# Five steps of a two-layer encoder are issued at other places of the program: the key scale's sum, the queries' root, the seam's spread, the next layer's normalized x, the last reciprocals

## The chip, the cores and the metric

The kernel runs on one core of a Trainium2 chip. The metric is the device time of one execution in microseconds (us), the median of three runs. A core has engines with instruction streams of their own: TensorE (PE in the profile, its weight loads apart as PEld), VectorE (DVE), ScalarE (ACT), GpSimd (POOL) and SyncE (SP), which here issues DMA transfers. Matmul results go to PSUM, all other tiles lie in SBUF. An engine runs its own instructions in order and waits on semaphores for what others produce.

## The reference

Two layers of an encoder over 1024 tokens of width 1024. What bears on the change is cut out here.

```python
for l in range(DEPTH):                                  # 2 layers
    h = _rmsnorm(x, g_mix[l])
    p = h @ w_in[l]                                     # 384 query, 256 key/value, 32 rotary, 2 x 512 conv columns
    c_q = _rmsnorm(p[..., :o1], g_q[l])
    q = (c_q @ w_uq[l]).reshape(b, s, 8, 64 + 32)       # 64 plain, 32 rotary
    c_kv = _rmsnorm(p[..., o1:o2], g_kv[l])
    kv = (c_kv @ w_ukv[l]).reshape(b, s, 8, 64 + 64)    # keys, values
    k_rope = _apply_rope(p[..., o2:o3], cos, sin)       # one rotary key for all heads
    y_attn = _mla_attention(q_nope, q_rope, k_nope, k_rope, v)   # softmax(q k / sqrt(96)) v
    a, gt = jnp.split(p[..., o3:], 2, axis=-1)
    u = _dwconv(a * jax.nn.sigmoid(gt), ...)            # 31 taps along the tokens
    u = jax.nn.silu(_layernorm(u, ...))
    x = x + jnp.concatenate([y_attn, u], -1) @ w_o[l]
    h2 = _rmsnorm(x, g_ffn[l])
    zg, zv = jnp.split(_dwconv(h2 @ w_up[l], ...), 2, axis=-1)   # 3 taps, 2 x 2816 columns
    x = x + (jax.nn.silu(zg) * zv) @ w_down[l]
return _rmsnorm(x, g_final)
```

## The kernel before

Activations lie transposed, with channels on the 128 partitions and tokens along a row of 1024 (two halves of 512, each one bank of PSUM). A value that needs more digits than one type holds is split into an upper and a lower half (names ending in h and l, or the two planes of one tile): ACT writes the upper half, DVE subtracts it and writes the lower, and PE multiplies three of the four combinations.

Per layer there are four stages: `project` (all products with `w_in`, and the keys and queries of all heads), `attention`, the product with `w_o`, and the channel mixer with an `up` and a `down` product. The order in which the code issues instructions is the order in which each engine runs them; no scheduler moves them afterwards.

`project` writes this order with a small planner. `seq` is a list of sections, each one product on PE: a1, g2, a2, g3, a3 (convolution inputs), kv0, kv1 (keys and values, latent), kr (rotary key), q0, q1, q2 (queries, latent), k0 to k3 (keys), u0, u1 (rotary queries), n0 to n3 (plain queries). For each section it issues the product, and then `work(until)` issues the work of DVE and ACT that belongs to earlier sections: it holds a clock of its own for DVE and one for PE, takes from the list `active` the generator whose time has come, and where none is due takes a step of the convolution (`taps`, L2172, one multiply and add over a whole row). A generator yields its cost on DVE and the delay until its next step is due. After that `after()` of the section runs, which can start further generators, and the section's own eviction is launched.

The names around the change, in `project`:

- `keys_norm` spreads the key root over the partitions by eight PE transposes (rkv0s, L342), ACT copies them (L736), and DVE multiplies the two latent key tiles `ckv` by them (L739); `parts` then splits these into kvs_0 and kvs_1, which are the input of the sections k0 to k3.
- `key_scale` adds a few squares over the partitions by a matmul with ones (kt, L628, two small matmuls), and makes a power of two of them in a short chain on DVE (tiles qk, the last at L636). Then it launches `key_rope_end`, which splits the rotary key (krs; ACT at L782, DVE at L784) and sends it to DRAM (krd) through SP. The eviction of k0 to k3 (`key`, tiles ks, ACT at L806, DVE at L808) needs the scale too.
- `query_latent` of q0, q1, q2 scales the product (cq, L720), squares it on ACT (qss, L728), adds the squares up on DVE (the first sum at L283, the second at L285), and splits it (cqs, L794 and L796).
- `root("qss", ...)` runs behind section k2 in layer 0 and behind k3 in layer 1: eight transposes of the sum of squares (rq0t, L304), after which DVE forms the reciprocal root (`roots`). `queries_norm` spreads it (rq0s and rq1s, L342) and multiplies cos and sin by it.
- `product(..., between={k: f})` calls f ahead of the k-th of its moving tiles; each tile stands for six matmuls.

Layer 1 begins with `next_sections`, the seam: products of the new layer run over the first half of the tokens, (g0, a0, g1) x 8 steps, while the second half is normalized: `norm_root` behind step 15, `norm_spread` (rx_512s) and eight `norm_apply` (x at L1863, split into xs by ACT at L1864 and DVE at L1852) behind step 20. The first half is normalized earlier, by `put(...)` steps among the last steps of layer 0's `down` product (pd, L1666), whose inputs ab are split at L1655 (ACT) and L1656 (DVE) at the same time. In `attention` the softmax sums of the last pair of heads are inverted (rc, L2051) and spread by transposes (rc_1s).

Of the kernel before, what the change touches and what calls it, by code (L numbers as in the profile page):

```python
# [26 lines left out]
QL = 384  # L27
# [120 lines left out]
class Encoder:  # L148
# [406 lines left out]
    def next_sections(self, l, nxt, supply):  # L555
        names = ("g0", "a0", "g1")
        supply(-30.0)
        w = [e[0] for e in nxt["ready"]]
        self.norm_sums(l, nxt["x"], nxt, 1, (7,))
        for i in (2, 1):  # L560
            self.pp.tile([128, T], F32, name=f"skip{l}{i}", tag=f"w{i}", bufs=1)
        ps = [self.wide(f"p{n}{l}") for n in names]
        tiles = [(lambda k, t=t: (t[:, 0, k], t[:, 1, k])) for t in w]
        order = [(i, k) for ks in (range(6), range(6, 8)) for i in range(2) for k in ks] + [(2, k) for k in range(8)]
        for n, (i, k) in enumerate(order):
            self.partial(ps[i], tiles[i], nxt["hl"], k, (0,))
            if n == 15:
                self.norm_root(l, nxt, 1, self.bank)
            if n == 20:
                self.norm_spread(l, nxt, 1, self.bank)  # L570
                for m in range(8):
                    self.norm_apply(l, nxt["x"], nxt, 1, m)
        for k in range(8):
            for i in range(3):
                self.partial(ps[i], tiles[i], nxt["hl"], k, (1,))
        supply(-16.0)
        return nxt["hl"], None, dict(zip(names, ps))
# [13 lines left out]
    def project(self, l, carry):  # L591
# [3 lines left out]
        taps, active, u, conv, away, far_at = [], [], {}, {}, {}, {}  # L595
# [78 lines left out]
        def start(steps, wait=1.8):  # L674
            next(steps)
            active.append([clock["pe"] + wait, steps, 99])
# [56 lines left out]
        def keys_norm():  # L733
            r = st["rkv"] = self.blk(f"rkv{l}")
            for s, p in zip(HALVES, self.spread(rooted("kroot"), f"rkv{l}", HALVES, self.bank)):
                nc.scalar.copy(out=r[:, s], in_=p)  # L736
            yield 0.0, 1.8
            for j in range(2):
                nc.vector.tensor_tensor(out=ckv[j], in0=ckv[j], in1=r, op=ALU.mult)  # L739
                yield 1.25, 0.0  # L740
            both = [parts(ckv[j], f"kvs{l}_{j}", kvs, par[:, P_GKV + j:P_GKV + j + 1]) for j in range(2)]
            yield [next(p) for p in both][0]
            for p in both:
                yield from p
# [43 lines left out]
        def query_latent(j):  # L788
            yield from latent(f"q{j}", cq, "qss", j)
            yield from parts(cq[j], f"cqs{l}_{j}", cqs, par[:, P_GQ + j:P_GQ + j + 1])  # L790
# [71 lines left out]
        def inputs(name):  # L862
            if l:
                between = {4: lambda: start(keys_norm(), 6.5), 7: lambda: start(key_scale(), 9.6)} if name == "q1" else {}
                return lambda: self.product(ps[name], lambda k: (w[name][:, 0, k], w[name][:, 1, k]), hl, between=between)
            return lambda: self.product(ps[name], self.tiled(w[name]), hl)

        def ranked(group, j, n, name, moving):
            def run():
                pair = tuple(t[:, j] for t in w[group])  # L870
                self.product(ps[name], lambda k: tuple(t[:, k * 128:(k + 1) * 128] for t in pair), moving)
            return run

        def root(key, out, n, name):
# [29 lines left out]
            add(f"kv{j}", f"kv{j}", inputs(f"kv{j}"), lambda j=j: latent(f"kv{j}", ckv, "kss", j))  # L904
        add("kr", "kr", shared_key, key_rope)
        add("q0", "q0", inputs("q0"), lambda: query_latent(0), lambda: root("kss", "kroot", KVL, "rkv"))
        add("q1", "q1", inputs("q1"), lambda: query_latent(1), None if l else lambda: (start(keys_norm()), list(key_scale())))
        add("q2", "q2", inputs("q2"), lambda: query_latent(2))
        between = {2 + l: lambda: root("qss", "qroot", QL, "rq")}
        norm = lambda: start(queries_norm())  # L910
# [1 line left out]
            add(f"k{j}", "k", ranked("k", j, KVL, f"k{j}", kvs), lambda j=j: key(j), between.get(j))  # L912
        for i in range(2):
            held = lambda: launch(query_rope(0), len(seq) - 6)
            add(f"u{i}", "u2", ranked("u2", i, QL, f"u{i}", cqs), lambda i=i: query_rope(1) if i else iter(()), held if i else norm)
        scales = {1: lambda: self.weight_squares(l, w["v"], sc),
                  2: lambda: (st.update(scale=self.scales(l, sc)))}
        for j in range(4):
# [2 lines left out]
        times, starts, t = {}, {}, 0.0  # L921
# [633 lines left out]
    def down_steps(self, l, steps, put):  # L1555
# [201 lines left out]
        put(n4 + 2, 4, lambda: sums(1, range(4)))  # L1757
        put(n4 + 3, 0.5, lambda: self.norm_spread(l + 1, nxt, 0, other))
        for k in range(8):
            put(n4 + 4 + k * 3 // 4 if not last else n4 + 3 + k // 2, 4, lambda k=k: self.norm_apply(l + 1, x, nxt, 0, k))  # L1760

        def resume():
            if not last:
# [150 lines left out]
    def attention(self, l, u, conv, away, spill, kvs, loaded, ahead, wo, begun):  # L1914
# [134 lines left out]
        def inverse(c):  # L2049
            r = self.cp.tile([128, 4], F32, name=f"rc{l}_{c}", tag="rc", bufs=2)  # L2050
            nc.vector.reciprocal(out=r, in_=state[HEADS - 1]["sums"][:, c * 4:c * 4 + 4])  # L2051
            return r
# [48 lines left out]
        agenda[56].append(lambda: sums(last - 1, slice(0, 64), state[last - 1], state[last - 1]["y"], state[last - 1]["rb"]))  # L2101
        agenda[60].append(lambda: [self.load_y(l, begun["x"], 0, k) for k in range(2)])
        for c, when in enumerate((60, 62)):
            agenda[when].append(lambda c=c: inv.update({c: inverse(c)}))
            agenda[when + 1].append(lambda c=c: spread(c, inv.pop(c)))
        self.last_pair = lambda: finish(last, state_y(), 1)
        for i in range(1, 4):
# [11 lines left out]
        for n in range(-2, total + 2):  # L2119
            if n == total - 2:  # L2120
                expo(n + 1)
            for g, c in chain.get(n, ()):
                values(g, c, n)
            if n == total - 1:
# [212 lines left out]
```

## Time and profile before

| | us |
|---|---|
| runs, median (lowest, highest) | 2170.31 (2170.06, 2170.36) |
| profiled execution | 2170.75 |
| its span, from the first to the last instruction | 2169.0 |
| PE busy | 2159.5 |
| DVE busy | 1853.8 |
| ACT busy | 1475.9 |
| POOL busy | 532.2 |
| mean granted clock of PE | 1.000 |

The span is what the trace covers; 1.75 us of the profiled execution lie around it. Rows of the timeline give the start of an instruction or of several alike, their time together, the engine, the line in the kernel, the operation, out<-in by the program's names, and the shape; in square brackets stands how long the engine was idle just ahead of it, and what released it. In the list of waits, a row gives the engine and line that waited, whom it waited for, and then us in total, how often, and the longest. SPq is the queue of SP's DMA issues.

### The profile page before, as it was taken

To read this page: it belongs to the slowest core of one execution; us is meant where nothing else is said; L and a number is where in the kernel's file an instruction comes from. 1 tells how busy PE (TensorE), PEld (TensorE's weight loads), DVE (VectorE), ACT (ScalarE), POOL (GpSimd) and SP (SyncE) were. 2 spreads that over 40 slices of the span, in tenths; PEclk is the share of its full clock that TensorE was granted. 3 is DMA by queue.
4 is the path that set the end of the run, shared out by engine and by line. 5 is a ranking of instruction groups with operands and counts; after the bars stand their busy time and mean duration, and the time that the engine had idled before them with its cause. 6 is when DMAs were issued, how large, how long until landed. Compare 5 with 4: busy or idle time off the path is not lost.

```text
span 2169.0 us, 29811 instructions
## 1 busy us (share of the span) xinstructions
PE 2159.5 (100%) x10726; PEld 1178.7 (54%) x10726; DVE 1853.8 (85%) x2554; ACT 1475.9 (68%) x2204; POOL 532.2 (25%) x518
## 2 busy tenths in 40 slices
PE   9999999999999999999999999999999999999998
PEld 8887565754444444444444576567544444444445
DVE  6989999879988887887978789988898888878877
ACT  6455888746898889554534668886478888865544
POOL 1233767311121111000001157890111111110000
PEclk9999999999999999999999999999999999999999
DMA  6898878854689899555345678896646988856533
GB/s 193 185 188 211 168 144 170 257 148 116 140 240 261 223 282 272 185 180 181 124 160 107 150 181 166 172 211 198 170 98 166 262 242 241 239 138 220 188 114 122
DMA packets 161508, 402.00 MB, mean 185 GB/s; under 512 B 19872, under 2 KB 27920, under 8 KB 161360
## 3 DMA queue, kind: packets, MB, share of 16 engines
q1 hardware_dynamic: 104080, 266.79, 35.9%
q0 software_dynamic: 56992, 132.78, 33.8%
q8 instruction: 84, 1.38, 0.2%
q14 instruction: 64, 0.52, 0.1%
q10 hardware_dynamic: 288, 0.53, 0.1%
HBM read 270.75 MB, written 69.66 MB: 157 GB/s over the span
## 4 chain that ended last, share of the span: by engine, by line
PE 97%; ACT 2%; DVE 1%; issue 0%; DMA 0%; SPq 0%; DVEq 0%; ACTq 0%
PE p L1392 36%; PE pd L1666 18%; PE po L1098 7%; PE s L1951 7%; PE t L1991 5%; PE pq L265 3%; PE pa L265 3%; PE o L2013 2%; PE pkv L265 2%; PE pg L265 2%; PE pg L588 2%; PE pn L265 2%; PE o L2018 1%; PE pv L1927 1%; PE pk L265 1%; PE pa L588 1%
## 5 line engine op out<-in xcount | busy, mean ns | idle before, releaser
L1392 PE MATMUL p<-b,w 128*128 128x512 f16 x3696 | 800.2, 379 | 0.3
L1392 PEld LDWEIGHTS <-w 128*128 128x128 f16 x3696 | 358.9, 98 | 431.6 <-issue 0.8
L1666 PE MATMUL pd<-ab,wd 128*128 128x512 f16 (+1 forms) x1920 | 401.0, 371 | 0.4 <-DVE ab L1656 0.4
L1268 POOL DMA_DIRECT2D wu<-in_w_up x176 | 152.8, 882 | 770.0 <-DVE w L1356 583.5
L1666 PEld LDWEIGHTS <-wd 128*128 128x128 f16 x1920 | 187.9, 98 | 210.7 <-issue 0.9
L1951 PE MATMUL s<-k,q 96*128 96x512 f16 x768 | 186.9, 379 | 0.0
L1356 DVE SCALAR_TENSOR_TENSOR w<-wu,wf,w 128x512 f16<-128x512 f32 (+1 forms) x216 | 177.1, 834 | 5.1 <-ACT w L1353 4.9
L1994 DVE SCALAR_TENSOR_TENSOR pt<-t,pt 128x512 f16<-128x512 f32 x256 | 163.0, 676 | 10.1 <-ACT pt L1993 9.1
L1353 ACT ACTIVATE w<-wu,wf 128x512 f16<-128x512 f32 (+1 forms) x216 | 164.9, 781 | 0.5 <-DMA wu<-in_w_up 0.4
L1993 ACT ACTIVATE pt<-t 128x512 f16<-128x512 f32 x256 | 139.2, 596 | 32.0 <-PE t L1991 30.1
L1953 DVE TENSOR_REDUCE mx<-s 128x1 f32<-128x1024 f32 x128 | 154.9, 1210 | 0.9 <-PE s L1951 0.9
L2189 POOL TENSOR_SCALAR late<-gate,par 128x1019 f32<-128x1019 f32 (+14 forms) x107 | 145.3, 1358 | 30.7 <-PE pn L265 30.7
L1655 ACT ACTIVATE ab<-ac,ds 128x512 f16<-128x512 f32 x108 | 75.5, 716 | 110.7 <-DVE ac L1561 78.3
L1961 ACT ACTIVATE p<-s,mx 128x1024 f32<-128x1024 f32 x128 | 143.3, 1119 | 2.2 <-DVE mx L1953 1.8
L1991 PE MATMUL t<-ident,p 128*128 128x128 f32 x1024 | 136.6, 275 | 0.9 <-ACT p L1961 0.6
L2172 DVE SCALAR_TENSOR_TENSOR conv<-gate,par,conv 128x1009 f32<-128x1009 f32 (+14 forms) x106 | 134.6, 1274 | 2.8 <-ACT conv L697 0.2
L1991 PEld LDWEIGHTS t<-ident,p 128*128 128x128 f32 x1024 | 116.8, 141 | 34.9 <-issue 7.4
L1899 DVE SCALAR_TENSOR_TENSOR o<-zg,par,o 128x1023 f32<-128x1023 f32 x88 | 112.7, 1281 | 9.9 <-ACT o L1893 8.4
L1899 DVE SCALAR_TENSOR_TENSOR v<-zv,par,v 128x1023 f32<-128x1023 f32 x88 | 112.1, 1276 | 1.4 <-ACT v L1893 1.4
L1400 DVE SCALAR_TENSOR_TENSOR zg<-p,wf,zg 128x512 f32<-128x512 f32 x72 | 54.0, 750 | 67.0 <-PE p L1392 54.2
L1951 PEld LDWEIGHTS <-q 96*128 96x128 f16 x768 | 74.1, 97 | 64.5 <-issue 2.1
L2179 POOL DMA_DIRECT2D conv<-far x27 | 23.3, 864 | 345.0 <-DVE conv L2172 289.2
(1536 smaller groups left out, 3714.0 us busy)
## 6 DMA issues: line engine op xcount, KB each, us to landing
wu<-in_w_up SPq DMA_DIRECT2D x98, 512.0 KB
wu<-in_w_up POOLq DMA_DIRECT2D x176, 256.0 KB, 5.1
sd<-in_w_down SPq DMA_DIRECT2D x44, 512.0 KB
ws<-sd SPq DMA_DIRECT2D x44, 512.0 KB
act<-v SPq DMA_DIRECT2D x36, 512.0 KB
ac<-act SPq DMA_DIRECT2D x72, 256.0 KB
wo<-in_w_o POOLq DMA_DIRECT2D x32, 256.0 KB, 7.7
x_mix<-y SPq DMA_DIRECT2D x32, 256.0 KB
```

What stands on the lines that cost most here:

```text
L265: nc.tensor.matmul(ps[:, HALVES[c]], w, x[:, HALVES[c]], start=(k == 0 and s == 0), stop=(k == n - 1 and s == 2))
L1098: self.nc.tensor.matmul(ps, p[:, sl], q[:, cs], start=(k == 0 and t == 0), stop=(k == 3 and t == 2))
L1268: nc.gpsimd.dma_start(out=dst, in_=src, accum_op=ALU.add)
L1353: nc.scalar.activation(out=t, in_=src, func=AF.Copy, scale=scale[f])
L1356: nc.vector.scalar_tensor_tensor(out=t, in0=src, scalar=scale[f], in1=hi, op0=ALU.mult, op1=ALU.subtract)
L1392: nc.tensor.matmul(ps, w[p][:, k * 128:(k + 1) * 128], b[:, q], start=(i in (1, 5, 2) and k == 0 and t == 0), stop=(k == 3 and t == 2), sk ...
L1666: nc.tensor.matmul(ps[t, m][:, cs], w[i, j][p][:, m * 128:(m + 1) * 128], b[:, q, cs], start=(i in (1, 5, 2) and j == 0 and s == 0), stop= ...
L1899: self.nc.vector.scalar_tensor_tensor(out=o[:, a:b], in0=z[:, at + a:at + b], scalar=self.par[l][:, tap:tap + 1], in1=o[:, a:b], op0=ALU.m ...
L1951: nc.tensor.matmul(ps[:, cs], q[0:96, i, qs], k[0:96, j, cs], start=(s == 0), stop=(s == 2))
L1953: nc.vector.tensor_reduce(out=mx, in_=ps, op=ALU.max, axis=AX.X, negate=True)
L1991: nc.tensor.transpose(tp[:, i, qi * 128:(qi + 1) * 128], st["p"][2 * qp + qi][:, kt * 128:(kt + 1) * 128], self.ident)
L1994: nc.vector.scalar_tensor_tensor(out=lo, in0=tp, scalar=P_SCALE, in1=hi, op0=ALU.mult, op1=ALU.subtract)
```

## The change

Instructions are neither added nor removed; they are issued at other places.

- Layer 0, `key_scale`: its matmul is issued inside q2's product, behind the first tile, instead of behind q1's product; it is drawn in one go there, ahead of the `work` of section q2.
- Layer 1, `queries_norm`: started inside u1's product, behind the first tile, instead of behind u0's.
- Layer 1's seam: `norm_spread` and the eight `norm_apply` behind step 19 instead of 20.
- The end of layer 0's `down`: the chunks k of the first half's `norm_apply` stand at step n4 + 4 + (k + 1) * 3 // 4 instead of n4 + 4 + k * 3 // 4, so that some come one step later.
- `attention`, both layers: the reciprocals of the second group of the last pair are issued behind the last `expo` instead of at step 62 of the agenda.

```diff
--- before.py
+++ after.py
@@ -566,7 +566,7 @@
             self.partial(ps[i], tiles[i], nxt["hl"], k, (0,))
             if n == 15:
                 self.norm_root(l, nxt, 1, self.bank)
-            if n == 20:
+            if n == 19:
                 self.norm_spread(l, nxt, 1, self.bank)
                 for m in range(8):
                     self.norm_apply(l, nxt["x"], nxt, 1, m)
@@ -863,12 +863,13 @@
             if l:
                 between = {4: lambda: start(keys_norm(), 6.5), 7: lambda: start(key_scale(), 9.6)} if name == "q1" else {}
                 return lambda: self.product(ps[name], lambda k: (w[name][:, 0, k], w[name][:, 1, k]), hl, between=between)
-            return lambda: self.product(ps[name], self.tiled(w[name]), hl)
-
-        def ranked(group, j, n, name, moving):
+            between = {1: lambda: list(key_scale())} if name == "q2" else {}
+            return lambda: self.product(ps[name], self.tiled(w[name]), hl, between=between)
+
+        def ranked(group, j, n, name, moving, between={}):
             def run():
                 pair = tuple(t[:, j] for t in w[group])
-                self.product(ps[name], lambda k: tuple(t[:, k * 128:(k + 1) * 128] for t in pair), moving)
+                self.product(ps[name], lambda k: tuple(t[:, k * 128:(k + 1) * 128] for t in pair), moving, between=between)
             return run
 
         def root(key, out, n, name):
@@ -904,7 +905,7 @@
             add(f"kv{j}", f"kv{j}", inputs(f"kv{j}"), lambda j=j: latent(f"kv{j}", ckv, "kss", j))
         add("kr", "kr", shared_key, key_rope)
         add("q0", "q0", inputs("q0"), lambda: query_latent(0), lambda: root("kss", "kroot", KVL, "rkv"))
-        add("q1", "q1", inputs("q1"), lambda: query_latent(1), None if l else lambda: (start(keys_norm()), list(key_scale())))
+        add("q1", "q1", inputs("q1"), lambda: query_latent(1), None if l else lambda: start(keys_norm()))
         add("q2", "q2", inputs("q2"), lambda: query_latent(2))
         between = {2 + l: lambda: root("qss", "qroot", QL, "rq")}
         norm = lambda: start(queries_norm())
@@ -912,7 +913,8 @@
             add(f"k{j}", "k", ranked("k", j, KVL, f"k{j}", kvs), lambda j=j: key(j), between.get(j))
         for i in range(2):
             held = lambda: launch(query_rope(0), len(seq) - 6)
-            add(f"u{i}", "u2", ranked("u2", i, QL, f"u{i}", cqs), lambda i=i: query_rope(1) if i else iter(()), held if i else norm)
+            add(f"u{i}", "u2", ranked("u2", i, QL, f"u{i}", cqs, {1: norm} if l and i else {}),
+                lambda i=i: query_rope(1) if i else iter(()), held if i else None if l else norm)
         scales = {1: lambda: self.weight_squares(l, w["v"], sc),
                   2: lambda: (st.update(scale=self.scales(l, sc)))}
         for j in range(4):
@@ -1757,7 +1759,7 @@
         put(n4 + 2, 4, lambda: sums(1, range(4)))
         put(n4 + 3, 0.5, lambda: self.norm_spread(l + 1, nxt, 0, other))
         for k in range(8):
-            put(n4 + 4 + k * 3 // 4 if not last else n4 + 3 + k // 2, 4, lambda k=k: self.norm_apply(l + 1, x, nxt, 0, k))
+            put(n4 + 4 + (k + 1) * 3 // 4 if not last else n4 + 3 + k // 2, 4, lambda k=k: self.norm_apply(l + 1, x, nxt, 0, k))
 
         def resume():
             if not last:
@@ -2101,7 +2103,8 @@
         agenda[56].append(lambda: sums(last - 1, slice(0, 64), state[last - 1], state[last - 1]["y"], state[last - 1]["rb"]))
         agenda[60].append(lambda: [self.load_y(l, begun["x"], 0, k) for k in range(2)])
         for c, when in enumerate((60, 62)):
-            agenda[when].append(lambda c=c: inv.update({c: inverse(c)}))
+            if c == 0:
+                agenda[when].append(lambda c=c: inv.update({c: inverse(c)}))
             agenda[when + 1].append(lambda c=c: spread(c, inv.pop(c)))
         self.last_pair = lambda: finish(last, state_y(), 1)
         for i in range(1, 4):
@@ -2119,6 +2122,7 @@
         for n in range(-2, total + 2):
             if n == total - 2:
                 expo(n + 1)
+                inv[1] = inverse(1)
             for g, c in chain.get(n, ()):
                 values(g, c, n)
             if n == total - 1:
```

On DVE in layer 0, from the key scale on, this stood before. Here ckv are the latent keys, cq the latent queries, qss the sum of their squares, conv a step of the convolution, and krs, kvs, cqs and ks the lower halves of splits.

```order
L784 SCALAR_TENSOR_TENSOR krs_1203<-krt_1058,qk_85,krs_1203 32x1024
L739 TENSOR_TENSOR ckv_932<-ckv_932,rkv_1175 128x1024
L739 TENSOR_TENSOR ckv_986<-ckv_986,rkv_1175 128x1024
L720 TENSOR_TENSOR cq_1273<-pq_1092,rx_380 128x1024
L2172 SCALAR_TENSOR_TENSOR conv_3_857<-gate_3_789,par_63,conv_3_857 128x1018
L796 SCALAR_TENSOR_TENSOR kvs_0l<-ckv_932,par_63,kvs_0h 128x1024
L796 SCALAR_TENSOR_TENSOR kvs_1l<-ckv_986,par_63,kvs_1h 128x1024
L283 SCALAR_TENSOR_TENSOR qss_1152<-qss_1152,qss_1_1275 128x1024
L720 TENSOR_TENSOR cq_1303<-pq_1207,rx_380 128x1024
L796 SCALAR_TENSOR_TENSOR cqs_1l<-cq_1273,par_63,cqs_1h 128x1024
L285 TENSOR_TENSOR qss_1152<-qss_1152,qss_2_1305 128x1024
L808 SCALAR_TENSOR_TENSOR ks_0_1327<-pk_1290,qk_85,ks_0_1327 128x1024
```

And this stands there now; ahead of the first row come a conv step and the first cq, right behind the scale.

```order
L739 TENSOR_TENSOR ckv_932<-ckv_932,rkv_1175 128x1024
L739 TENSOR_TENSOR ckv_986<-ckv_986,rkv_1175 128x1024
L283 SCALAR_TENSOR_TENSOR qss_1152<-qss_1152,qss_1_1264 128x1024
L2176 SCALAR_TENSOR_TENSOR conv_3_857<-gate_3_789,par_63,conv_3_857 128x1019
L796 SCALAR_TENSOR_TENSOR kvs_0l<-ckv_932,par_63,kvs_0h 128x1024
L796 SCALAR_TENSOR_TENSOR kvs_1l<-ckv_986,par_63,kvs_1h 128x1024
L796 SCALAR_TENSOR_TENSOR cqs_1l<-cq_1262,par_63,cqs_1h 128x1024
L784 SCALAR_TENSOR_TENSOR krs_1278<-krt_1058,qk_85,krs_1278 32x1024
L720 TENSOR_TENSOR cq_1305<-pq_1194,rx_380 128x1024
L808 SCALAR_TENSOR_TENSOR ks_0_1324<-pk_1292,qk_85,ks_0_1324 128x1024
L2176 SCALAR_TENSOR_TENSOR conv_3_857<-gate_3_789,par_63,conv_3_857 128x1020
L285 TENSOR_TENSOR qss_1152<-qss_1152,qss_2_1307 128x1024
```

The split krs moved behind that of cqs_1, the first sum at L283 moved forward, and the second sum at L285 now stands behind the lower half of ks and a further conv step.

On ACT, the pair of q2's square and the splits of cqs_2 and ks, before (wor is a weight whose squares are summed, wu10 a weight's split):

```order
L620 ACTIVATE wor_3b,sc_86<-wor_3b 128x1024
L728 ACTIVATE qss_2_1305<-cq_1303 128x1024
L794 ACTIVATE cqs_2h<-cq_1303,par_63 128x1024
L806 ACTIVATE ks_0_1327<-pk_1290,qk_85 128x1024
L226 ACTIVATE wu10l<-wu10h 128x768
```

And now:

```order
L620 ACTIVATE wor_3b,sc_86<-wor_3b 128x1024
L728 ACTIVATE qss_2_1307<-cq_1305 128x1024
L806 ACTIVATE ks_0_1324<-pk_1292,qk_85 128x1024
L794 ACTIVATE cqs_2h<-cq_1305,par_63 128x1024
L226 ACTIVATE wu10l<-wu10h 128x768
```

The upper half of ks changed places with that of cqs_2.

On DVE at the end of layer 0's `down` product, where x is the residual stream being normalized, xs its lower half, and ab the lower half of `down`'s input, before:

```order
L1863 SCALAR_TENSOR_TENSOR x_0_8287<-x_0_8287,wz,rx_9671 128x512
L1863 SCALAR_TENSOR_TENSOR x_1_8309<-x_1_8309,wz,rx_9671 128x512
L1852 TENSOR_TENSOR xs_0_9697<-x_0_8287,xs_0_9697 128x512
L1656 SCALAR_TENSOR_TENSOR ab_47_9716<-v_18_7768,ds_4022,ab_47_9716 128x512
L1863 SCALAR_TENSOR_TENSOR x_2_8342<-x_2_8342,wz,rx_9671 128x512
L1852 TENSOR_TENSOR xs_1_9700<-x_1_8309,xs_1_9700 128x512
L1656 SCALAR_TENSOR_TENSOR ab_48_9735<-v_19_7928,ds_4022,ab_48_9735 128x512
```

And now:

```order
L1865 SCALAR_TENSOR_TENSOR x_0_8287<-x_0_8287,wz,rx_9671 128x512
L1658 SCALAR_TENSOR_TENSOR ab_47_9712<-v_18_7768,ds_4022,ab_47_9712 128x512
L1865 SCALAR_TENSOR_TENSOR x_1_8309<-x_1_8309,wz,rx_9671 128x512
L1854 TENSOR_TENSOR xs_0_9697<-x_0_8287,xs_0_9697 128x512
L1658 SCALAR_TENSOR_TENSOR ab_48_9731<-v_19_7928,ds_4022,ab_48_9731 128x512
L1658 SCALAR_TENSOR_TENSOR ab_49_9734<-v_20_8063,ds_4022,ab_49_9734 128x512
L1658 SCALAR_TENSOR_TENSOR ab_410_9737<-v_21_8221,ds_4022,ab_410_9737 128x512
```

Each split ab stands behind one chunk of x fewer than before.

## Prediction

> **What bounds the kernel now.** I read the page first, its engines and its chain of waits, and then the list of PE's waits.
>
> ```profile
> PE 2159.5 (100%) x10726; PEld 1178.7 (54%) x10726; DVE 1853.8 (85%) x2554; ACT 1475.9 (68%) x2204; POOL 532.2 (25%) x518
> PE 97%; ACT 2%; DVE 1%; issue 0%; DMA 0%; SPq 0%; DVEq 0%; ACTq 0%
> PE pd L1666 <- DVE ab L1656: 0.4, 1, 0.4
> ```
>
> PE is busy for 2159.5 of 2169.0 us and carries 97% of the chain that ends last. After the program's first microseconds its longest single wait is the third row, 0.4 us. The number of instructions doesn't change, and neither does the order on POOL or SP. So the change can gain only the waits it removes, each a fraction of a microsecond, and can lose as much as any new wait of PE lasts. With PE this full, a microsecond that PE waits anywhere is a microsecond of the span. I therefore looked up each of the five places in the timeline, with PE and the engine that PE waits for there, and asked what is late afterwards.
>
> **The change part by part. Key scale's sum, layer 0.** The timeline around it, PE with DVE and ACT:
>
> ```profile
> 146.77 1.03 PE L342 MATMUL rkv0s<-ident,rkv0y 128*128 128x128 f32 x8
> 148.10 0.38 PE L628 MATMUL kt<-qk,ones_r 128*128 128x3 f32 x2 [0.29 <-ACT rkv L736]
> 151.41 0.15 DVE L636 TENSOR_SCALAR qk<-qk 128x1 f32<-128x1 f32 x1
> 152.59 1.27 DVE L784 SCALAR_TENSOR_TENSOR krs<-krt,qk,krs 32x1024 f16<-32x1024 f32 x1 [1.03 <-ACT krs L782]
> 153.79 2.34 DVE L739 TENSOR_TENSOR ckv<-ckv,rkv 128x1024 f32<-128x1024 f32 x2
> 156.06 1.21 DVE L720 TENSOR_TENSOR cq<-pq,rx 128x1024 f32<-128x1024 f32 x1
> 157.19 1.26 DVE L2172 SCALAR_TENSOR_TENSOR conv<-gate,par,conv 128x1018 f32<-128x1018 f32 x1
> 158.38 1.27 DVE L796 SCALAR_TENSOR_TENSOR kvs_0l<-ckv,par,kvs_0h 128x1024 fp32r<-128x1024 f32 x1
> 159.58 1.27 DVE L796 SCALAR_TENSOR_TENSOR kvs_1l<-ckv,par,kvs_1h 128x1024 fp32r<-128x1024 f32 x1
> 160.78 1.21 DVE L283 SCALAR_TENSOR_TENSOR qss<-qss,qss 128x1024 f32<-128x1024 f32 x1
> 163.04 1.26 DVE L796 SCALAR_TENSOR_TENSOR cqs_1l<-cq,par,cqs_1h 128x1024 fp32r<-128x1024 f32 x1
> 163.15 1.06 ACT L728 ACTIVATE qss<-cq 128x1024 f32<-128x1024 f32 x1 [1.63 <-DVE cq L720]
> 164.12 1.14 ACT L794 ACTIVATE cqs_2h<-cq,par 128x1024 fp32r<-128x1024 f32 x1
> 164.25 1.23 DVE L285 TENSOR_TENSOR qss<-qss,qss 128x1024 f32<-128x1024 f32 x1
> 165.16 1.09 ACT L806 ACTIVATE ks<-pk,qk 128x1024 f16<-128x1024 f32 x1
> 166.28 1.28 DVE L808 SCALAR_TENSOR_TENSOR ks<-pk,qk,ks 128x1024 f16<-128x1024 f32 x1 [0.81 <-ACT ks L806]
> 167.49 1.04 PE L304 MATMUL rq0t<-ident,qss 128*128 128x128 f32 x8
> 168.29 0.70 PE L265 MATMUL pk<-kvs_0h,wk0h 128*128 128x512 f32 x2
> 153.89 0.33 SPq L156 DMA_DIRECT2D krd<-krs  x1
> 167.60 0.34 SPq L156 DMA_DIRECT2D kd<-ks  x1
> ```
>
> Gain: eight transposes (rkv0s) start at 146.77, and the next matmul 1.33 later. Behind the like eight of rq0t (167.49) the next comes after 0.80. So moving kt away from there gives 1.33 − 0.80 = 0.53 us; kt's own time on PE is only moved. Its reader, the small chain on DVE that ends at 151.56 (151.41 + 0.15), is held by DVE's earlier work, since kt is over before 149.5 even behind six matmuls of q2.
>
> Loss: the order on DVE behind that chain changes. In the steps between starts of the rows above, it is now a conv step (157.19 to 158.38: 1.19), the first cq (156.06 to 157.19: 1.13), two ckv (2.27), the first qss sum (1.13, taken as the cq), a conv step (1.19), two kvs splits (158.38 to 160.78: 2.40), the cqs_1 split (1.20) and only then the krs split (1.20). That is 11.71: from 151.55 to 163.26. Then cq2 (1.21) ends at 164.47. ACT squares it (its step 163.15 to 164.12: 0.97) and now writes the upper half of ks ahead of cqs_2's (1.09): ready at 166.5 to 166.6. DVE stands in front of the lower half of ks for that long, about 2.1 us, because this now comes ahead of the second qss sum. The split takes 1.20 (to 167.8), another conv step 1.19 (to 169.0), and the second qss sum 1.23: it ends at 170.2 to 170.3, where before it ended at 165.48.
>
> PE's rq0t needs that sum. It started at 167.49 without waiting, 2.0 us behind it. Now PE is due there at 167.49 − 0.53 = 166.96, at most at 167.3 if small waits ahead of it (kvs_0's lower half comes a little later than PE's product with it) take back some of the 0.53. It starts at 170.2 to 170.4, taken as 170.34: later than before by **2.85 us**, in a wait of about 3.1 to 3.3. Bounds: with the DVE rows back to back at their whole durations (thirteen rows by about 0.07 more) the sum ends 0.9 later, and the loss is 3.8; if the sum were ready in time, there is the gain of 0.53 alone. I take 2.85, since every step in it is a row of this same stretch. The krs DMA on SP leaves about 9.5 later (163.4 instead of 153.89); behind it SP next issues at 167.60, so nothing queues there. The two ks splits end within 0.3 us of their old time, so its DMA is not late either.
>
> **Normalized x at the end of layer 0's down product.**
>
> ```profile
> 1068.32 8.15 PE L1666 MATMUL pd<-ab,wd 128*128 128x512 f16 x37
> 1074.10 1.28 ACT L1864 CAST xs<-x 128x512 f16<-128x512 f32 x2 [2.06 <-DVE x L1863]
> 1075.29 0.72 ACT L1655 ACTIVATE ab<-v,ds 128x512 f16<-128x512 f32 x1
> 1076.04 0.75 DVE L1656 SCALAR_TENSOR_TENSOR ab<-v,ds,ab 128x512 f16<-128x512 f32 x1 [0.60 <-ACT ab L1655]
> 1076.84 10.47 PE L1666 MATMUL pd<-ab,wd 128*128 128x512 f16 x47 [0.38 <-DVE ab L1656]
> 1100.06 0.16 DVE L320 SCALAR_TENSOR_TENSOR rx_512y<-rx_512q,rx_512y 128x4 f32<-128x4 f32 x1
> 1101.18 0.60 PE L342 MATMUL rx_512s<-ident,rx_512y 128*128 128x128 f32 x4
> 1101.62 2.11 PE L588 MATMUL pg<-xs,wg1s 128*128 128x512 f16 x9
> 1103.89 0.38 PE L588 MATMUL pg<-xs,wg0s 128*128 128x512 f16 x1 [0.17 <-ACT xs L1864]
> 1104.62 0.59 PE L588 MATMUL pg<-xs,wg0s 128*128 128x512 f16 x2 [0.35 <-DVE xs L1852]
> ```
>
> A matmul takes 0.216 here: nine span 2.11 and one alone 0.38, (2.11 − 0.38) / 8. So 37 from 1068.32 make PE due at 1076.31, and it starts at 1076.84: 0.53 lost, since the lower half of ab waits for ACT's upper half, which stands behind two casts of xs. Now one cast stands there: ab is ready half of 1.28, 0.64, earlier, so the wait goes. A second, like step two chunks later may give 0.1. I take **−0.6**; the bounds are −0.65 and 0, the latter if DVE, not ACT, is late there. What is delayed, the normalized chunks, is read first by the next layer's products more than 20 us later.
>
> **Seam's spread, layer 1.** Nine from 1101.62 are due to end at 1103.56; PE goes on at 1103.89. One matmul behind it, the next is due 0.216 later, yet starts at 1104.62: 1104.62 − 1103.56 − 0.216 = 0.84 lost, to the casts and subtractions of xs behind the spread. The spread (rx_512s) moves three matmuls forward, 0.65. Its input is ready at 1100.22 (1100.06 + 0.16) and the spread is due at 1101.18 − 0.65 = 1100.53: still in time. All that follows moves by 0.65, less what DVE and ACT can't follow: **−0.63**, at most −0.65, at least 0.
>
> **Queries' root, layer 1, and the last reciprocals.**
>
> ```profile
> 1246.33 0.61 PE L265 MATMUL pu<-cqs_2l,wu21h 128*128 128x512 f32 x2
> 1247.20 1.06 PE L342 MATMUL rq1s<-ident,rq1y 128*128 128x128 f32 x8 [0.26 <-DVE rq1y L320]
> 392.46 1.29 DVE L1994 SCALAR_TENSOR_TENSOR pt<-t,pt 128x512 f16<-128x512 f32 x2
> 393.66 0.17 DVE L2051 RECIPROCAL rc<-sums 128x4 f32<-128x4 f32 x1
> 393.98 0.62 PE L342 MATMUL rc_1s<-ident,rc 128*128 128x128 f32 x4
> ```
>
> Two matmuls of pu step by 2 × 0.225, which makes rq1s due at 1246.78; it starts at 1247.20, 0.42 later. Put six matmuls further on, about 1.3 us, it finds the root ready: **−0.42** (−0.42 to −0.26, by the wait in the row). The multiplications of cos and sin behind it come a microsecond later, and nothing on PE is due for them at once. The last reciprocal is over at 393.83 and its spread starts at 393.98. Issued earlier it is out of the way, but PE then stands behind DVE's two pt (over at 393.75), from whose bank of PSUM the spread follows; with the 0.05 to 0.15 from DVE to PE seen here and at 1076.84, that is 0.0 to 0.2 earlier: **−0.1 in each layer, −0.2** (−0.5 to 0 in both).
>
> **The sum.** 2.85 − 0.60 − 0.63 − 0.42 − 0.20 = **+1.0**. Profiled, 2170.75 (span 2169.0 and 1.75 around it) becomes 2171.75; the median of the runs is 0.44 below the profiled execution, 2170.31, so it becomes **2171.3**. With the bounds of the first term from 2.3 to 3.4 and the others as they stand, 2170.4 to 2172.2. Less than 0.2%, 4.3 us, can hardly be told from no change here.
>
> **The rivals.** *The order on DVE costs nothing.* If the second qss sum were ready when PE comes, only gains are left: −0.53 − 0.60 − 0.63 − 0.42 − 0.20 = −2.4, 2167.9. It would have to end 3.3 us sooner than my steps say, and only 2.1 us of them are waiting. 8%.
>
> *The gains don't come.* The waits at the down product, the seam and the root are each bound by two engines; if the next instruction is as late as the old one, only +2.85 stays: 2173.1. The margins above (0.31 at the spread) speak against it. 8%.
>
> *The stall lowers PE's clock, and the change is slower.* The only place of this trace where PE rests that long is its end, in windows (length, busy time of five engines, granted clock, DMA):
>
> ```profile
> 2165.00:2167.00 2.00, 0.00 (x0) 0.00 (x0) 0.00 (x0) 0.00 (x0) 0.00 (x0) 1.00 0.98 357
> 2167.00:2168.00 1.00, 0.00 (x0) 0.00 (x0) 0.00 (x0) 0.00 (x0) 0.00 (x0) 0.62 0.56 211
> ```
>
> PE is idle from before 2165.0, and the clock is full until 2167.0 and falls within the next microsecond: 0.62 there, the mean of 1 and one half, means at 2167.24. So more than 2.2 us of rest are needed, and the new wait is 3.1 to 3.3, followed by 0.8 us of transposes. If the clock halves and full speed returns after a stretch as long as the wait, half of 3.3 is lost, +1.7: 2173.0. If it takes two stretches, +3.5 comes on top of +1.0: 2174.8, slower than before by 0.2%. [...] 5% for the first, 3% for the second.
>
> [...]
>
> **How the numbers follow.** The sum as it stands has 76%, the rivals 8% (2167.9), 8% (2173.1), 5% (2173.0) and 3% (2174.8). The range runs from 2169.5 to 2173.1: it leaves out the gains-only case and the far clock case, and holds the others. None of the first four differs by 0.2% (2166.0 and 2174.7 are the marks), so same has 96%, slower 3%, faster 1% for gains larger than any wait shown.
>
> **What would show it.** Right: PE idle about 3 us ahead of rq0t, released by DVE's second qss sum; DVE idle about 2 us ahead of the lower half of ks, released by ACT; no wait ahead of kt, pd's 0.4 gone, pg's waits together at most 0.2, no wait at rq1s; granted clock 1.00 at 170 to 175. Wrong: rq0t without a wait, a granted clock below 1 behind it, or pd and pg waiting as before.

## The result, and the profile after

The changed kernel takes 2174.21 us in the median of 15 runs (2172.81 to 2175.14), against 2170.31 in 15 runs of the kernel before (2170.0 to 2170.79): a ratio of 1.0017, 95% interval 1.0009 to 1.0025. It is slower by 3.9 us, about 0.18%, where the prediction said +1.0. The profiled execution took 2174.18, 3.43 more than that of before, with a span of 2172.4.

The page's busy times and chain by engine, of the kernel after:

```profile
PE 2160.4 (99%) x10726; PEld 1179.2 (54%) x10726; DVE 1856.9 (85%) x2554; ACT 1476.0 (68%) x2204; POOL 535.4 (25%) x518
PE 97%; ACT 1%; DVE 1%; issue 0%; DMA 0%; SPq 0%; DVEq 0%; ACTq 0%
```

PE's work is nearly what it was (0.9 more), so most of the loss is waiting. DVE and POOL are each about 3 us busier with the same instructions: some of them must last longer. PE's waits, after:

```profile
PE rq0t L304 <- DVE qss L285: 2.7, 1, 2.7
...
PE s L1953 <- ACT p L1963: 0.8, 1, 0.8
...
PE pv L1929 <- DVE v L1942: 0.4, 1, 0.4
```

The first was predicted. The waits at kt, pd, pg and rq1s in the middle of the program are gone. Two new ones stand at the start of layer 0's attention, where nothing was predicted. The timeline of the stretch with the first wait, PE, DVE and ACT, after:

```profile
162.87 1.20 DVE L720 TENSOR_TENSOR cq<-pq,rx 128x1024 f32<-128x1024 f32 x1
164.10 1.06 ACT L728 ACTIVATE qss<-cq 128x1024 f32<-128x1024 f32 x1 [3.16 <-DVE cq L720]
165.07 1.09 ACT L806 ACTIVATE ks<-pk,qk 128x1024 f16<-128x1024 f32 x1
166.20 1.28 DVE L808 SCALAR_TENSOR_TENSOR ks<-pk,qk,ks 128x1024 f16<-128x1024 f32 x1 [2.13 <-ACT ks L806]
166.52 0.61 PE L265 MATMUL pk<-kvs_1l,wk0h 128*128 128x512 f32 x2
167.40 1.27 DVE L2176 SCALAR_TENSOR_TENSOR conv<-gate,par,conv 128x1020 f32<-128x1020 f32 x1
168.59 1.22 DVE L285 TENSOR_TENSOR qss<-qss,qss 128x1024 f32<-128x1024 f32 x1
169.86 1.97 PE L304 MATMUL rq0t<-ident,qss 128*128 128x128 f32 x8 [2.73 <-DVE qss L285]
171.48 1.20 PE L265 MATMUL pk<-kvs_0h,wk0h 128*128 128x512 f32 x2
172.48 0.77 PE L265 MATMUL pk<-kvs_0h,wk0l 128*128 128x512 f32 x2
```

The chain is the one that was worked out: cq, ACT's square, ks on ACT, 2.13 us of idle DVE, ks on DVE, a conv step, the sum. But look at the eight transposes: 1.97 us, where the same eight took 1.04. And the pair of matmuls behind them takes 1.20 instead of 0.70. The granted clock of this stretch, in windows (length, busy times of PE, PEld, DVE, ACT and POOL, clock, DMA share, GB/s), after:

```profile
166.00:168.00 2.00, 1.14 (x6) 0.60 (x4) 1.80 (x2) 2.00 (x4) 0.00 (x0) 1.00 0.05 12
168.00:170.00 2.00, 0.14 (x1) 0.14 (x2) 2.00 (x3) 1.94 (x2) 1.18 (x1) 0.84 0.88 311
170.00:172.00 2.00, 2.00 (x9) 1.96 (x10) 2.00 (x2) 0.00 (x0) 0.00 (x0) 0.50 0.96 192
172.00:174.00 2.00, 2.00 (x8) 1.60 (x7) 1.90 (x6) 0.00 (x0) 0.00 (x0) 0.81 1.10 211
```

While PE rested, its clock fell, to 0.50 in the third window. Taken as one fall and one rise, 0.84 puts the fall at 169.36, 2.2 us behind the last matmul (166.52 + 0.61), and 0.81 the rise at 172.76: 3.4 us at half speed, 2.9 of them with work.

Then the start of layer 0's attention, after: DVE, POOL and PE.

```profile
200.75 1.23 DVE L840 TENSOR_TENSOR qn<-pn,rq 128x1024 f32<-128x1024 f32 x1 [2.26 <-PE pn L265]
201.89 3.26 DVE L844 SCALAR_TENSOR_TENSOR qns<-qn,qns 128x1024 f16<-128x1024 f32 x1
205.07 3.19 DVE L844 SCALAR_TENSOR_TENSOR qns<-qn,qns 128x1024 f16<-128x1024 f32 x2
201.68 2.39 POOL L2196 TENSOR_TENSOR conv<-conv,late 128x1020 f32<-128x1020 f32 x1
204.05 3.15 POOL L2193 TENSOR_SCALAR late<-gate,par 128x1020 f32<-128x1020 f32 x1
209.20 0.47 PE L1929 MATMUL pv<-wv0h,kvs_0h 128*128 128x512 f32 x1 [0.41 <-DVE v L1942]
213.04 1.46 PE L1953 MATMUL s<-k,q 96*128 96x512 f16 x6 [0.83 <-ACT p L1963]
```

And the kernel before at the same place, with one more split from layer 1 in the last row:

```profile
198.87 1.28 DVE L2172 SCALAR_TENSOR_TENSOR conv<-gate,par,conv 128x1022 f32<-128x1022 f32 x1
200.12 1.23 DVE L844 SCALAR_TENSOR_TENSOR qns<-qn,qns 128x1024 f16<-128x1024 f32 x1
200.70 0.89 POOL L2194 DMA_DIRECT2D conv<-late  x1 [5.25 <-issue]
202.84 2.35 POOL L2192 TENSOR_TENSOR conv<-conv,late 128x1020 f32<-128x1020 f32 x1
1271.37 2.18 DVE L844 SCALAR_TENSOR_TENSOR qns<-qn,qns 128x1024 f16<-128x1024 f32 x1 [1.11 <-ACT qns L842]
```

A split of a query, which reads two tiles of SBUF, takes 1.23 before. After, the first of three takes 3.26 and the other two 3.19 together: 1.21, and 2.05 for the last, from 206.21 on. POOL's addition beside the first took 2.39 against 2.35 before; the POOL step behind it, of a kind that takes 1.11 to 1.48 elsewhere in this attention, took 3.15. Before, POOL's DMA into conv came behind DVE's conv step at 198.87, and POOL's addition at 202.84 behind the last split. After, that conv step stood earlier on DVE (at 178.84), POOL was let go earlier, and its addition fell on the splits.

Last, the four other places after: one unbroken row of 84 matmuls at the end of the down product, the seam, rq1s, and the spread of the last reciprocals.

```profile
1073.71 18.34 PE L1668 MATMUL pd<-ab,wd 128*128 128x512 f16 x84
1105.27 0.60 PE L342 MATMUL rx_512s<-ident,rx_512y 128*128 128x128 f32 x4
1108.29 1.00 PE L588 MATMUL pg<-xs,wg0s 128*128 128x512 f16 x3
1252.21 1.03 PE L342 MATMUL rq1s<-ident,rq1y 128*128 128x128 f32 x8
399.38 0.65 PE L342 MATMUL rc_1s<-ident,rc 128*128 128x128 f32 x4
```

None of them shows an idle time of PE in brackets any more.

How far the same instruction of PE lies behind its time in the kernel before gives a ledger: −0.30 at rkv0s (146.47 against 146.77), a lead from the first 25 us of the program, where no edit is; −0.51 at the last product ahead of rq0t (166.52 against 167.03), +2.37 where rq0t starts, +3.78 at the fourth matmul behind the transposes (172.85 against 169.06), +5.46 at the third group of scores (213.04 against 207.58), +5.57 late in this attention (355.69 against 350.12), +5.40 at the last reciprocals (399.38 against 393.98), +4.73 behind the down product, +4.08 behind the seam, +3.59 behind rq1s (1253.54 against 1249.95), +3.42 at layer 1's last reciprocals. So the wait cost 2.88 from start to start (2.73 of them idle), the low clock 1.41, the start of attention 1.68; the four other edits returned about 0.67, 0.65, 0.49 and 0.34. A lead like the 0.30 is no effect of the change: at rkv0s the traces of the kernels here lie between 0.81 earlier and 0.34 later than the kernel before.

### The profile page after: what moved, and what is told of

It is laid out like the page before. It is cut to its first block, busy times and chain, and to the rows that moved or that the text cites. A ratio compares the mean times of both kernels' runs of the same rounds, so it can differ in the third digit from the quotient of the medians.

```text
span 2172.4 us, 29809 instructions
## 1 busy us (share of the span) xinstructions
PE 2160.4 (99%) x10726; PEld 1179.2 (54%) x10726; DVE 1856.9 (85%) x2554; ACT 1476.0 (68%) x2204; POOL 535.4 (25%) x518
## 4 chain that ended last, share of the span: by engine, by line
PE 97%; ACT 1%; DVE 1%; issue 0%; DMA 0%; SPq 0%; DVEq 0%; ACTq 0%
PE p L1394 36%; PE pd L1668 18%; PE po L1100 7%; PE s L1953 7%; PE t L1993 5%; PE pa L265 3%; PE pq L265 3%; PE o L2015 2%; PE pkv L265 2%; PE pg L265 2%; PE pg L588 2%; PE pn L265 2%; PE o L2020 1%; PE pa L588 1%; PE pv L1929 1%; PE pu L265 1%
```

## The experiments

The theory that came from this (theory 1 below): all loss comes from the first edit, by the order on DVE that follows it, in three terms, wait, clock and collision. The rivals were that other edits cost too, that the low clock belongs to the place and not to the wait, and that DVE is late at attention by its order and not by POOL. Every kernel was timed in five rounds beside the kernel before (medians of 2170.35 to 2170.41).

**One edit undone, and that edit alone.** First, the sum of layer 0 stands behind q1's product again; then, the reverse, that edit alone on the kernel before.

```diff
-            between = {1: lambda: list(key_scale())} if name == "q2" else {}
-            return lambda: self.product(ps[name], self.tiled(w[name]), hl, between=between)
+            return lambda: self.product(ps[name], self.tiled(w[name]), hl)
...
-        add("q1", ..., None if l else lambda: start(keys_norm()))
+        add("q1", ..., None if l else lambda: (start(keys_norm()), list(key_scale())))
```

> The changed kernel with the first of its five edits undone: the key scale's sum stands behind q1's product again. Theory 1 (the loss comes from this edit alone, by the order on DVE that follows it): no wait at rq0t, no fall of PE's clock at 170, no wait at the start of attention, and the four other edits gain what the shifts of PE's instructions between the two traces show: -0.7 at the down product, -0.65 at the seam, -0.55 at the queries' root, -0.25 at the reciprocals, together about -2.2: 2168.1 us. Rival (the other edits cost too, and the wait at the start of attention is theirs, by the reciprocals' order): 2169.5 or more.

Measured: 2168.24 us, ratio 0.9991 (0.9982 to 1.0000). Its trace has no wait at rq0t, pv or s, and a clock of 1.00 from 164 to 174.

> The kernel before with the first edit alone. Theory 1: the stall at rq0t, the low clock behind it and the waits at the start of attention all stand here without the gains: 2174.2 + 2.2 = 2176.4 us, within 0.7. Rival (part of the loss belongs to the other edits): under 2175.

Measured: 2176.57 us, ratio 1.0028 (1.0017 to 1.0039). Its waits of PE:

```profile
PE rq0t L304 <- DVE qss L285: 2.7, 1, 2.7
...
PE s L1952 <- ACT p L1962: 0.9, 1, 0.9
...
PE pv L1928 <- DVE v L1941: 0.4, 1, 0.4
```

And its clock in windows:

```profile
170.00:172.00 2.00, 1.63 (x10) 1.53 (x11) 2.00 (x3) 0.45 (x1) 0.00 (x0) 0.81 1.01 232
172.00:174.00 2.00, 2.00 (x6) 1.52 (x6) 1.97 (x4) 0.00 (x0) 0.00 (x0) 0.50 1.04 174
174.00:176.00 2.00, 2.00 (x9) 1.62 (x8) 1.80 (x8) 0.10 (x1) 0.36 (x1) 0.83 0.73 272
```

All three terms come with this one edit, and the other four gain 2.2 together. (PE also waits 0.7 for the lower half of kvs_0 here, a wait that is 0.2 or less in the other traces.) By the same reckoning the clock fell at 171.24 and rose at 174.68: again 3.4 us at half speed, but the fall came 3.6 us behind the last matmul (167.04 + 0.61) and 0.87 behind the start of the transposes at 170.37, where in the changed kernel it came 2.2 behind the last matmul.

**Each of the four others alone** on the kernel before, each the diff's own lines.

> The kernel before with the seam's spread and normalized x one step earlier alone. By the steps of the prediction: -0.63, 2169.7 us; if the gain needs the others, 2170.3.

> The kernel before with the normalized x at the end of the down product one step later alone. By the steps of the prediction: -0.6, 2169.7 us, no wait of 0.4 at pd; if another engine is late there, 2170.3.

> The kernel before with the queries' root spread inside u1's product in layer 1 alone. By the steps of the prediction: -0.42, 2169.9 us, no wait at rq1s; if the later cos and sin make PE wait, 2170.3 or more.

> The kernel before with the last reciprocals issued earlier alone. By the steps of the prediction: -0.2, 2170.1 us (-0.5 to 0); nothing that can be told from 2170.3 if PE waits for the bank all the same.

Measured: 2169.84, 2169.67, 2169.85 and 2170.19 us beside 2170.41 and (the last three) 2170.35: −0.57, −0.68, −0.50, −0.16. Each ratio alone has 1 in its interval (0.9997, 0.9988 to 1.0006, for the seam); together they are −1.9, against −1.85 in the prediction and −2.2 in the kernel without the first edit.

**The place of the sum without the order.** The rotary key's split is issued at once behind the scale; every row on DVE and ACT then stands as in the kernel before.

```diff
-            between = {1: lambda: list(key_scale())} if name == "q2" else {}
+            between = {1: lambda: (list(key_scale()), finish(-1))} if name == "q2" else {}
```

> The changed kernel, with the split of the rotary key issued at once behind the scale, so that the order on DVE and ACT is that of the kernel before and only the two small matmuls of the sum have moved on PE. Theory 1 (the place of the sum on PE is worth 0.5, and what costs is the order on DVE): 0.5 below the kernel without the edit: 2167.6 us, no wait at kt nor at rq0t. Rival (the sum costs PE as much inside q2's product as ahead of it): the same as without the edit, 2168.1.

Measured: 2167.91 us, ratio 0.9989 (0.9980 to 0.9998), the fastest version here. PE at this place:

```profile
146.70 1.03 PE L342 MATMUL rkv0s<-ident,rkv0y 128*128 128x128 f32 x8
147.49 0.70 PE L265 MATMUL pq<-xs_0h,wq20h 128*128 128x512 f32 x2
148.95 0.28 PE L628 MATMUL kt<-qk,ones_r 128*128 128x3 f32 x2
159.66 0.73 PE L265 MATMUL pk<-kvs_0l,wk0h 128*128 128x512 f32 x2
167.06 1.04 PE L304 MATMUL rq0t<-ident,qss 128*128 128x128 f32 x8
```

The wait at kt is gone (0.79 from rkv0s to the next matmul) and rq0t waits for nothing. Against the kernel without the edit the median is 0.33 lower; the two ranges overlap (2167.66 to 2169.09 and 2167.97 to 2169.05), so the runs support the gain of 0.5 in sign and not in size. The trace shows where the rest of it went: PE lies 0.07 ahead of the kernel before at rkv0s and 0.63 ahead at the first pk (158.70 against 159.33), but 0.45 three pairs later (160.24 against 160.69) and 0.43 at rq0t, since the pair in the fourth row starts late and takes 0.73 instead of 0.62. So 0.56 was gained at kt and 0.2 of it handed back to the lower half of kvs_0.

**The clock.** Eleven matmuls that nobody reads fill the wait; they write the bank that the transposes then overwrite.

```diff
             ps = bank(name + "t")
+            for _ in range(11 if fill and not out else 0):
+                self.nc.tensor.matmul(ps, *fill, start=True, stop=True)
```

> The changed kernel with eleven matmuls of 128x512 ahead of rq0t, about 2.5 us that nobody reads, in the time in which PE waits for the second sum of squares. Theory 1 (the wait halves PE's clock, and this costs 1.4 beside the wait): clock 1.00 from 166 to 176, the eight transposes in 1.0 instead of 2.0, 1.4 less than the changed kernel: 2172.8 us, with less spread between runs. Rival (the low clock belongs to the transposes or to that place, or the matmuls add to the wait): 2174.2 or more.

Measured: 2173.49 us (2172.64 to 2174.11), 0.72 under the changed kernel. The timeline of this kernel:

```profile
167.72 2.65 PE L304 MATMUL rq0t<-kvs_0h,wk0h 128*128 128x512 f32 x11
170.58 1.09 PE L306 MATMUL rq0t<-ident,qss 128*128 128x128 f32 x8 [0.20 <-DVE qss L285]
```

And a window, with the clock third from the end:

```profile
170.00:172.00 2.00, 1.79 (x13) 1.34 (x12) 2.00 (x3) 0.67 (x1) 0.13 (x1) 1.00 0.99 260
```

The transposes take 1.09 and the clock stays at 1.00 (from 160 to 178). This one trace doesn't yet clear the transposes or the place, because kernels with the whole rest keep their clock in some executions too, as the next runs show; two rows of the table at the end of this section do. From the second transpose to the fourth matmul behind them PE regains 1.2 us against the trace of the changed kernel; the median, 2173.49, lies between the 2172.8 of theory 1 and the 2174.2 of the rival. The traced execution, 2174.11, is hardly faster than that of the changed kernel, 2174.18, for two reasons that its trace shows. It was 0.64 later at rkv0s (147.11 against 146.47), ahead of any edit. And it lost 0.56 at 847 us, in the first `up` product:

```profile
PE p L1397 <- ACT zg L1404: 0.4, 1, 0.4
```

ACT had waited 0.91 there for the transfer of a weight, against 0.26 in the changed kernel. The traces of all three kernels with such matmuls lose something at this place (0.56, 0.15 and 0.32), the others here nothing; whether the matmuls cause it isn't shown.

**The collision.** The convolution's last step on DVE is held back to where it stood before; the wait at rq0t stays.

```diff
-                if at is None and taps and clock["dve"] + TAP <= until:
+                if at is None and taps and (l or len(taps) > 1 or until > 1e8) and clock["dve"] + TAP <= until:
```

> The changed kernel, with the last step of layer 0's convolution on DVE held back until the last query section, so that DVE's order from the query root on is that of the kernel before (the last plain query behind two splits, then the convolution's step, then the last split), while the stall at rq0t stays. Theory 1 (in the changed order two splits of queries, which read two tiles of SBUF, fall on POOL's convolution steps and last 3.26 and 2.05 us instead of 1.22, and PE waits for this at the start of attention): all splits 1.2, no wait of PE at pv and s, 1.7 less: 2172.5 us. Rival (DVE is simply late by the stall and PE waits anyway): 2174.2.

Measured: 2172.78 us (2171.01 to 2173.37), 1.4 less, where 1.7 was forecast. The timeline is of the fastest of these runs:

```profile
169.68 1.09 PE L304 MATMUL rq0t<-ident,qss 128*128 128x128 f32 x8 [2.73 <-DVE qss L285]
196.85 3.04 DVE L844 SCALAR_TENSOR_TENSOR qns<-qn,qns 128x1024 f16<-128x1024 f32 x2
202.20 1.22 DVE L844 SCALAR_TENSOR_TENSOR qns<-qn,qns 128x1024 f16<-128x1024 f32 x1
204.92 2.35 POOL L2196 TENSOR_TENSOR conv<-conv,late 128x1020 f32<-128x1020 f32 x1
```

Its clock behind the wait:

```profile
170.00:172.00 2.00, 2.00 (x14) 1.75 (x12) 2.00 (x3) 0.00 (x0) 0.00 (x0) 1.00 0.91 179
```

The last split takes 1.22, POOL's addition comes behind it, and PE's waits at pv and s are gone. The two splits ahead take 3.04 together and not the forecast 2.4, with a POOL step of 1.15 at 196.55 beside the first; PE doesn't wait for them. Here PE rested 2.73 us as in the changed kernel, and the clock did not fall (1.00 from 164 to 174). The runs lie in two groups, four from 2171.0 to 2171.6 and seven from 2172.7 to 2173.4, as they would if the price of the clock were paid in some executions and not in others; only one of the first group was traced. To tell POOL's work from DVE's order, POOL's steps of the convolution in layer 0's attention are left out, with DVE in the changed order:

> The changed kernel without the convolution steps that POOL does in layer 0's attention (these taps are left out of the sum), with everything else in its order. Theory 1 (it is POOL's work beside the splits that lengthens them): the splits take 1.2 each although DVE's order is the changed one, and the waits at pv and s go or fall to a few tenths: 2172.5 us, or less where DVE is eased elsewhere in attention. Rival (the order of the last query ahead of two splits alone makes DVE late): the splits 1.2, but PE still waits over 1 us at the start of attention: 2173.5 or more.

Measured: 2173.12 us (2171.04 to 2173.92), between the 2172.5 of theory 1 and the 2173.5 of the rival, so the time alone doesn't decide. DVE in its trace, which is of the fastest run and has the clock at 1.00 from 164 to 174:

```profile
199.02 1.22 DVE L840 TENSOR_TENSOR qn<-pn,rq 128x1024 f32<-128x1024 f32 x1 [2.26 <-PE pn L265]
200.16 3.49 DVE L844 SCALAR_TENSOR_TENSOR qns<-qn,qns 128x1024 f16<-128x1024 f32 x3
```

DVE still idles 2.26 us for the last query, with the same three splits behind it. They take 3.49 together instead of 6.4, and PE waits neither at pv nor at s. So POOL's work beside the splits was the cause here, and the rival falls by the trace: DVE's order alone costs PE nothing there. Why the median lies 0.6 above the forecast stays open.

**Both mended, and a shorter rest.** The last two kernels have the tail's order back, and eleven or five matmuls in the wait.

> The changed kernel with both: eleven matmuls that nobody reads in the wait, and the tail's order back. If the clock and the collision are the two terms that the prediction lacked, this comes to the time that was predicted without them: 2171.3 us, within 0.6. If there is a third, it stays above 2172.5.

> The changed kernel with the tail's order back and five matmuls that nobody reads instead of eleven in the wait: PE rests about 1.6 us instead of 0.2 or 2.7. In the traces so far PE rested 2.7 us four times without such matmuls, and its clock fell twice. Theory 1 (a rest of about half the 3.6 us in which the clock fell at the program's end is too short for a fall): clock 1.00 in the trace, and the runs lie as those with eleven matmuls do, median 2171.8 within 0.4. Rival (any rest over a microsecond risks it): a part of the runs lies 1.4 higher, as in the kernel with the tail's order back and no such matmuls (2172.8).

Measured: 2171.83 us (2171.39 to 2172.89) and 2171.49 (2171.09 to 2172.25). Without clock and collision the changed kernel is within 0.5 and 0.2 of the predicted 2171.3. PE's longest wait in the kernel with five:

```profile
PE rq0t L306 <- DVE qss L285: 1.6, 1, 1.6
```

And its window:

```profile
170.00:172.00 2.00, 2.00 (x14) 1.78 (x14) 2.00 (x2) 0.00 (x0) 0.00 (x0) 1.00 0.93 191
```

A rest of 1.6 us left the clock alone in this trace (1.00 from 164 to 174), and the runs reach no higher than with eleven. Of four traces with a rest of 2.7 us, two have the fall (the changed kernel and the first edit alone) and two don't. The falls and rises of the changed kernel are read from windows of 0.01 us, those of the first edit alone from its windows of 2 us:

| kernel | rest of PE | clock |
|---|---|---|
| changed | 167.14 to 169.86 | falls at 169.35, 2.21 behind the start of the rest; full again at 172.76 |
| first edit alone | 167.65 to 170.37 | falls at 171.24, 3.59 behind the start of the rest; full again at 174.68 |
| tail's order back | 166.96 to 169.68 | 1.00 from 164 to 174 |
| POOL's steps left out | 166.77 to 169.49 | 1.00 from 164 to 174 |
| five matmuls | 168.27 to 169.86 | 1.00 from 164 to 174 |

At the program's end the clock falls 3.56 us behind PE's last matmul in the kernel before (2167.23 against 2163.67) and 2.47 behind it in the changed kernel (2169.56 against 2167.09). The transposes and the place are the same in all four kernels with a rest of 2.7 us, and two of these keep their clock, so neither the place nor the transposes lower it by themselves; nor does the length of the rest, which is the same in the four to 0.01 us. What sets the two pairs apart isn't shown.

## Why the prediction was wrong

- *The order on DVE and the wait at rq0t*: right, step for step. The sum was to end at 170.2 to 170.3 and ended at 169.81, or 170.1 without the lead of 0.30. PE was due 0.21 earlier than before by the change itself, since small waits took back most of the gain at kt, which the prediction allowed for; so an idle 2.73 came where 3.1 to 3.3 was forecast, and rq0t starts 2.67 later, without the lead, where 2.85 was forecast. The idle 2.1 us ahead of the lower ks was 2.13.
- *The clock*: this is the rival that came true, with a price of 1.41 in the trace against 1.7. It was given 8% in both its forms. The step that failed is the reading of the program's end: that PE's clock stood at 1.00 up to 2167.0 was taken as a reason for which a rest of 3.1 would mostly pass, although the same rows allowed a fall from 2.2 us on. "More than 2.2 us of rest are needed" doesn't follow from one fall either, which in fact came 3.6 us behind PE's last matmul (over at 2163.67). What the runs showed in its place: with a rest of 2.7 us, the falls came 2.2 us after the last matmul in one trace and about 3.6 in the other (171.24 against 167.65), and not at all in two more, so the length of the rest doesn't tell whether a single run pays. The 3.5 of the rival's second form is shown by no run: both traces with the fall have 3.4 us at half speed, one stretch and not two.
- *No cost on POOL*: the failed step that was not among the rivals. "The order on POOL doesn't change" was right, and was taken to mean that nothing there changes. What moved is when DVE's conv step releases POOL. The price was 1.68. The row that could have told it, the split of 2.18 at 1271.37, with POOL's step of 1271.03 (1.44) and its addition of 1272.55 (3.23) beside it, stood in the trace of before.
- *The four gains*: −0.60, −0.63, −0.42 and −0.20 were forecast; alone they measure −0.68, −0.57, −0.50 and −0.16. The gain at kt was put at 0.53 and measures 0.33 where it stands without the order, within the spread of the runs; the trace has 0.56 at kt and 0.2 handed back.
- *The sum*: +1.0 was forecast; with the missing 1.41 + 1.68, and 0.2 less for the wait (2.67 instead of 2.85), it is +3.9, by which the medians differ. The profiled executions differ by 3.4, because that of the changed kernel had the lead of 0.30 and its four gains come to 2.15 instead of 1.85. The bounds given beside the sum don't come out of its terms: 2.3 and 3.4 less 1.85 make 2170.8 and 2171.9, not 2170.4 and 2172.2.

Not every overlap with POOL cost the same. In the changed kernel the first and the last of the three splits took 3.26 and 2.05 us against 1.23 before, while the middle one (from 205.07) took 1.21, with POOL's step of 3.15 (from 204.05) beside it; the multiplication of qn, whose one input is in PSUM, took 1.23 at 200.75 beside a POOL step of 1.42 (from 200.18).

## What to carry to other kernels

Moving one small instruction in code that plans its own order moves everything behind it: read the new order of the engine that feeds the bottleneck, and keep that order fixed while the small thing moves, as the fastest version here does. A wait of PE of 2.7 us had a second price, its clock, in two of four traces (1.41 us in that of the changed kernel); matmuls that nobody reads, which fill the wait or cut it to 1.6 us, avoided it in the traces here. One trace can therefore not tell whether a wait of this length costs more than itself. An engine whose order is unchanged can still run at another time: ask what releases it and which instructions it will then lie beside.

## What the runs showed of the hardware

In two of four traces with a rest of PE of 2.7 us its clock fell to half, 2.2 and 3.6 us behind the last matmul, and stayed there 3.4 us each time; in the two others it stayed at 1.00, and so it did in one trace with a rest of 1.6 us. At the program's end it fell 3.56 us behind the last matmul in the kernel before and 2.47 in the changed one. Splits of queries, which read two tiles of SBUF, took 3.26, 1.21 and 2.05 us beside POOL's convolution steps, and 3.49 together where these steps were left out; one POOL step beside them took 3.15 instead of 1.11 to 1.48, while POOL's addition took 2.39 against 2.35. The spread of the runs is no safe sign of the clock: it is 2.3 us for the changed kernel, but 1.25 in seven runs of the first edit alone, whose trace has the fall, and 1.4 for the fastest version, whose trace has none.
